# Attention of a hybrid layer: a third PSUM bank for the transposed probabilities, one bank for z and the way out, and their additions, statistics and shifts as steps of their own

## The chip, the cores and the metric

The kernel runs on one core of a Trainium2 chip. The metric is device time in microseconds (us), from the first to the last instruction of one execution and what lies around it; lower is better. Times of single instructions come from one profiled execution. A core has a matrix engine (PE, TensorE, with its weight loads shown apart as PEld), three engines for element-wise work (DVE = VectorE, ACT = ScalarE, POOL = GpSimd), and SP, whose queue issues most of the transfers. Matrix products land in PSUM, which has eight banks of 128 rows by 512 float32; DVE and ACT read them there.

## What is computed

One layer of a decoder, 1024 tokens of width 1024, float32:

```python
x = layer_norm(DN_ALPHA * x + 0.5 * swiglu(x, ffn1_wg[i], ffn1_wu[i], ffn1_wd[i]), ln1_g[i], ln1_b[i])
proj = x @ w_in[i]
o_gdn = gdn_mixer(g_q, g_k, g_v, g_z, g_b, g_a, ...)          # ends in o * rsqrt(...) * norm_w * silu(z)
o_nsa = nsa_mixer(n_q, n_kc, n_vc, n_ks, n_vs, n_kw, n_vw, n_gate, ...)
mix = jnp.concatenate([o_gdn, o_nsa], axis=-1) @ w_out[i]
x = layer_norm(DN_ALPHA * x + mix, ln2_g[i], ln2_b[i])
x = layer_norm(DN_ALPHA * x + 0.5 * swiglu(x, ffn2_wg[i], ffn2_wu[i], ffn2_wd[i]), ln3_g[i], ln3_b[i])
```

`nsa_mixer` is attention with 8 query heads of width 64 and 2 key heads, in three branches whose gated results are added: over 63 compressed blocks of keys, over all earlier keys (16 selected blocks of 64 are all blocks there are), and over a window of 512 keys. Each branch has its own softmax.

## The kernel before, in words

The kernel runs the first feed-forward part, then `project` (the projections and the gated DeltaNet), then `attend`, then the second feed-forward part. The change lies in `attend`, which does three things at once: the attention (`nsa_tile`), the z projection of the DeltaNet's gate (`z_blocks`), and the way out, that is the gate, the product with `w_out`, the residual and the statistics of the second layer norm (`tile_out`).

All float32 products are made of three products of rounded parts (a high part times both, a low part times the high one), so one step of z or of the way out is three matrix products of 128x512 (lines 1047 and 1093).

**The attention.** It goes through 8 tiles of 128 tokens, from the last (t = 7) to the first, and for each through two key heads (kv = 0, 1): 16 groups. A group has 1 + 8 or more units. A unit of the compressed branch makes scores of 4 heads against 64 blocks (lines 1658 and 1662); a unit of the other two branches makes the scores `sc` of one head against up to 512 keys (lines 1704 and 1705, and a mask at 1707), DVE takes their negated maximum `nm` (line 1709), and ACT the exponentials `pr` with their sum (line 1710). Scores have three banks. After the last unit of a branch DVE works out the factors `f` (lines 1720 to 1735) and POOL scales `pr` by them (line 1738), eight instructions for a group's branch. Some slots later come the branch's parts, one for each 128 keys: PE turns the probabilities of four heads round into the bank `pt` (line 1628, four products), ACT copies its high part `th` (line 1632), DVE the low part `tl` (line 1635), and PE adds both products with the values to `po` (line 1641). Then `po` is copied out (`ov`, line 1752), swapped by two transfers (`sw`) and added into the tile's output `o` by POOL (line 1761).

**The order.** `slot` puts one unit and one part together: first the turning of a part, then a unit's scores, then the low part and the exponentials, then the values' products of the part before. Between slots `run` takes steps of a filler at a fixed rate per group (line 1201). The filler is a generator, first `z_blocks`, then `tile_out(7)`, `tile_out(6)` and so on, each two tiles behind the attention; a step ends at each `yield`. When a tile's attention is through, for t below 6, the rest of the filler is run at once (line 1202). PE's order is the program's; the other engines' instructions are put in order by a scheduler that goes by what is ready and by the program's order. Each engine runs its own list in that order.

**z.** 8 blocks of 8 steps, each into a bank `pr` of the pool `zps`, which has two. After the eighth step ACT takes the tanh (line 1055), DVE forms (tanh + 1) * z (line 1056), ACT scales (line 1057) and SP stores it. These four have no step of their own: they are in the step that starts the next block.

**The way out.** `tile_out` loads the DeltaNet's output and z, POOL multiplies them (line 1071), ACT and DVE split the tile's output into `oh` and `ol` (line 1082, in `split`, lines 100 and 103), and PE makes two halves of eight steps each, again in the two banks of `zps`. DVE adds the residual to a half (line 1101), in the step after the first step of the next half. After the last step come one `yield`, the second addition, one more `yield`, and then in one go `ln_rows` (line 745): two `bn_stats`, `bn_aggr`, the reciprocal root `rstd` (DVE, then POOL, lines 108 and 110) and the shift `nmr` (DVE, line 749), which needs POOL's root. The eight banks are: `po` one, `pt` two, scores three, `zps` two.

## Time and profile before

| | |
|---|---|
| time, median of 3 runs | 2138.01 us (2135.66 to 2139.01) |
| the profiled execution's own time | 2137.25 us |
| its span, first to last instruction | 2135.3 us |
| PE, matrix products, busy in the span | 2074.9 us (97%) |
| DVE / ACT / POOL busy in the span | 1514.9 / 923.0 / 586.4 us |
| `attend` runs from about 1069 to 1475 us | 406 us |
| in it PE / DVE / ACT / POOL busy | 386.74 / 279.95 / 242.19 / 157.60 us |

PE's ends are modelled and its products overlap, so its busy time is read as an upper bound; what counts is how far one product starts after the other, and the idle time that the profile puts before a product with the instruction that ended it. That is a term in square brackets in the rows below. A product of 128x512 of the same kind starts 0.23 us after the one before where nothing holds it.

### The profile page before, as it was taken

To read this page: it belongs to the slowest core of one execution; us is meant where nothing else is said; L and a number is where in the kernel's file an instruction comes from. 1 tells how busy PE (TensorE), PEld (TensorE's weight loads), DVE (VectorE), ACT (ScalarE), POOL (GpSimd) and SP (SyncE) were. 2 spreads that over 40 slices of the span, in tenths; PEclk is the share of its full clock that TensorE was granted. 3 is DMA by queue.
4 is the path that set the end of the run, shared out by engine and by line. 5 is a ranking of instruction groups with operands and counts; after the bars stand their busy time and mean duration, and the time that the engine had idled before them with its cause. 6 is when DMAs were issued, how large, how long until landed. Compare 5 with 4: busy or idle time off the path is not lost.

```text
span 2135.3 us, 29714 instructions
## 1 busy us (share of the span) xinstructions
PE 2074.9 (97%) x10247; PEld 1712.8 (80%) x10247; DVE 1514.9 (71%) x2644; ACT 923.0 (43%) x1956; POOL 586.4 (27%) x608
## 2 busy tenths in 40 slices
PE   9999999999999999999999999999999999999998
PEld 7788888888887887888878777777788888887886
DVE  7867767587888648635557677765976556569998
ACT  6333333344443334245356666655533323334441
POOL 2544444200023013000014344442244444320011
PEclk9999999999999999999999999999999999999999
DMA  4345555198624524576455411122333223259761
GB/s 145 123 151 180 201 174 197 46 359 265 222 74 152 159 76 162 155 215 192 122 146 180 158 65 55 61 75 85 103 109 123 94 85 118 80 194 339 232 201 55
DMA packets 251384, 316.46 MB, mean 148 GB/s; under 512 B 25393, under 2 KB 154530, under 8 KB 251234
## 3 DMA queue, kind: packets, MB, share of 16 engines
q1 hardware_dynamic: 246498, 298.05, 42.9%
q0 software_dynamic: 4736, 16.52, 2.0%
q8 instruction: 81, 1.33, 0.3%
q14 instruction: 69, 0.57, 0.1%
HBM read 219.08 MB, written 93.32 MB: 146 GB/s over the span
## 4 chain that ended last, share of the span: by engine, by line
PE 38%; DVE 5%; issue 3%; DMA 2%; POOL 1%; ACT 1%; POOLq 0%; SPq 0%; DVEq 0%; ACTq 0%
PE bk L299 16%; PE dn L627 8%; PE pr L1093 4%; PE po L1641 3%; PE pt L1628 3%; PE pr L1047 2%; PE sc L1705 1%; PE sc L1704 1%; DVE tl L1635 1%; POOL pr L1738 1%; DVE st L278 0%; DVE wl L285 0%; DMA ba<-in_ln_b_dram 0%; PE sc L1707 0%; DMA zw<-zw 0%
## 5 line engine op out<-in xcount | busy, mean ns | idle before, releaser
L299 PE MATMUL bk<-x,wh 128*128 128x512 f32 x1040 | 325.1, 394 | 6.0 <-ACT wh L284 4.2
L627 PE MATMUL dn<-bl,ah 128*128 128x512 f32 x616 | 240.4, 390 | 1.2 <-DVE bl L103 1.2
L627 PE MATMUL dn<-bh,ah 128*128 128x512 f32 x616 | 239.9, 389 | 0.0
L627 PE MATMUL dn<-bh,al 128*128 128x512 f32 x616 | 239.8, 389 | 0.0
L299 PEld LDWEIGHTS bk<-x,wh 128*128 128x128 f32 x1040 | 196.7, 190 | 49.4 <-ACT wh L284 5.6
L299 PE MATMUL bk<-acc,wh 128*128 128x512 f32 x704 | 217.0, 389 | 0.4 <-ACT ev L233 0.2
L299 PE MATMUL bk<-t,wh 128*128 128x512 f32 x704 | 216.8, 389 | 0.0
L284 ACT CAST wh<-st 128x512 fp32r<-128x512 f32 x176 | 108.3, 622 | 240.9 <-PE bk L299 204.9
L299 PE MATMUL bk<-x,wl 128*128 128x512 f32 x520 | 204.8, 394 | 2.1 <-DVE wl L285 2.0
L356 POOL TENSOR_TENSOR ev<-ev 128x512 f32<-128x512 f32 x80 | 132.0, 1652 | 152.0 <-ACT wh L284 65.4
L100 ACT CAST ah<-raw 128x512 fp32r<-128x512 f32 x154 | 95.2, 622 | 175.5 <-PE dn L627 89.4
L284 ACT CAST wh<-wraw 128x512 fp32r<-128x512 f32 x130 | 80.3, 623 | 182.9 <-PE bk L299 172.3
L1738 POOL TENSOR_SCALAR pr<-pr,f 128x512 f32<-128x512 f32 (+3 forms) x192 | 106.8, 575 | 182.9 <-DMA zw<-zw 41.4
L299 PEld LDWEIGHTS bk<-acc,wh 128*128 128x128 f32 x704 | 132.0, 188 | 28.2 <-ACT ev L233 0.4
L299 PEld LDWEIGHTS bk<-t,wh 128*128 128x128 f32 x704 | 132.1, 188 | 27.5
L278 POOL TENSOR_TENSOR st<-wraw 128x512 f32<-128x512 f32 x76 | 101.0, 1329 | 183.8 <-DVE wl L285 151.7
L1709 DVE TENSOR_REDUCE nm<-sc 128x1 f32<-128x512 f32 (+3 forms) x192 | 99.2, 519 | 72.2 <-PE sc L1707 68.6
L285 DVE TENSOR_TENSOR wl<-wraw,wh 128x512 fp32r<-128x512 f32 x130 | 118.3, 914 | 36.0 <-ACT wh L284 36.0
L627 PEld LDWEIGHTS dn<-bl,ah 128*128 128x128 f32 x616 | 115.6, 188 | 27.1 <-DVE bl L103 3.2
L299 PE MATMUL bk<-acc,wl 128*128 128x512 f32 x352 | 136.9, 389 | 0.0
L299 PE MATMUL bk<-t,wl 128*128 128x512 f32 x352 | 136.9, 389 | 0.0
L627 PEld LDWEIGHTS dn<-bh,ah 128*128 128x128 f32 x616 | 115.7, 188 | 23.9
(390 smaller groups left out, 4783.6 us busy)
## 6 DMA issues: line engine op xcount, KB each, us to landing
raw<-h SPq DMA_DIRECT2D x154, 256.0 KB
raw<-in_ffn_wd_dram SPq DMA_DIRECT2D x154, 256.0 KB
h<-ev SPq DMA_DIRECT2D x140, 256.0 KB
wraw<-in_ffn_wg_dram SPq DMA_DIRECT2D x20, 1024.0 KB
wraw<-in_ffn_wu_dram SPq DMA_DIRECT2D x20, 1024.0 KB
wraw<-in_w_in_dram SPq DMA_DIRECT2D x20, 512.0 KB
acc<-in_x_dram SPq DMA_DIRECT2D x32, 256.0 KB
wo<-ev SPq DMA_DIRECT2D x32, 256.0 KB
```

Source lines behind the costliest of these rows:

```text
L100: nc.scalar.copy(hi, src)
L278: (e or u.adder).tensor_tensor(t, a, b, op=o)
L284: nc.scalar.copy(h, src)
L285: nc.vector.tensor_tensor(l, src, h.bitcast(F32), op=ALU.subtract)
L299: nc.tensor.matmul(ps, w[:, kc, :], v[kc], start=(kc == 0 and i == 0), stop=(kc == 3 and i == 2))
L356: (nc.vector if u.f + 2 == NF else nc.gpsimd).tensor_tensor(t, t, u.gate.g[i, j], op=ALU.mult)
L627: nc.tensor.matmul(ps, a[:, t * P:(t + 1) * P], w, start=start and i == 0, stop=stop and i == 2)
L1093: nc.tensor.matmul(pp, a[:, kc, :], w[u][:, kc, :], start=(kc == ks[0] and i == 0), stop=(kc == ks[-1] and i == 2))
L1628: nc.tensor.transpose(pt[:keys, h, :], pr()[:, h, c:c + keys], self.ident)
L1641: nc.tensor.matmul(po[0], v, w[:keys], start=(first and w is th[0]), stop=(last and w is tl[0]))
L1709: nc.vector.tensor_reduce(nm[:, j, h:h + 1], ps[:, :w], axis=AX.X, op=ALU.max, negate=True)
L1738: nc.gpsimd.tensor_scalar(prs[j][:, h, :], prs[j][:, h, :], f[:, j, h:h + 1], 1.0, op0=ALU.mult, op1=ALU.mult)
```

## The change

Five things are done. `zps` loses a bank and `npt` (the pool of `pt`) gains one. In `z_blocks` the four instructions behind a block become four steps (`finish`: the tanh, an empty step, DVE's product, the scaling with the store), so that a new block starts five steps after the last one ended. In `tile_out`, for tiles 7 to 2, a half's addition is a step of its own right behind its eighth step, and an empty one follows; the first half's `bn_stats` comes behind the first step of the second half. After the second half's addition come two empty steps, its `bn_stats`, the aggregate with the root, and the shift, a step each. `ln_rows` is cut into `ln_stats` and `ln_shift` for that. Tiles 1 and 0, which run when the attention is over, keep the addition one step behind and take a score bank for their second half. The rates of the filler rise, since there are more steps: from 20, 15, 15 and 14 to 28, 23, 23 and 22 for the first four groups, from 10 to 13 for the others.

```diff
--- before.py
+++ after.py
@@ -743,8 +743,10 @@
 
 
     def ln_rows(self, a, st=None, eps=LN_EPS):
+        return self.ln_shift(a, *self.ln_stats(a, st, eps))
+
+    def ln_shift(self, a, mv, rstd):
         nc = self.nc
-        mv, rstd = self.ln_stats(a, st, eps)
         nmr = self.cpool.tile([P, 1], F32, name="nmr", bufs=3)
         nc.vector.scalar_tensor_tensor(nmr, mv[:, 0:1], -1.0, rstd, op0=ALU.mult, op1=ALU.mult)
 
@@ -1012,10 +1014,10 @@
             self.nqs, self.npp = pool("nqs", bufs=2), pool("np", bufs=2)
             op, zp = pool("op", bufs=2), pool("zp", bufs=2)
             self.prs = Ring(*[(p, "pr") for p in reversed(prs)])
-            self.npo, self.npt = pool("npo", bufs=1, space=PSUM), pool("npt", bufs=2, space=PSUM)
-            sa, sb = pool("nsa", bufs=1, space=PSUM), pool("nsc", bufs=1, space=PSUM)
+            self.npo, self.npt = pool("npo", bufs=1, space=PSUM), pool("npt", bufs=3, space=PSUM)
+            sb, sa = pool("nsc", bufs=1, space=PSUM), pool("nsa", bufs=1, space=PSUM)
             self.nps = Ring((sb, "s0"), (sb, "s1"), (sa, "s2"))
-            self.zps = pool("zps", bufs=2, space=PSUM)
+            self.zps = pool("zps", bufs=1, space=PSUM)
             oT, fin = {}, {}
 
             loads = []
@@ -1037,6 +1039,17 @@
                     return w
 
                 w = [load(0, k) for k in range(2)]
+
+                def finish(u, b, pp):
+                    z = zp.tile([P, 512], F32, name="z", padded_shape=[P, T])
+
+                    def out():
+                        nc.scalar.mul(z, z, self.nw)
+                        nc.sync.dma_start(self.zT[b][:, u * 512:u * 512 + 512], z)
+
+                    return [lambda: nc.scalar.activation(z, pp, AF.Tanh), lambda: None,
+                            lambda: nc.vector.scalar_tensor_tensor(z, z, 1.0, pp, op0=ALU.add, op1=ALU.mult), out]
+
                 for n in range(8):
                     u, b = divmod(n, 4)
                     pp = self.zps.tile([P, 512], F32, name="pr")
@@ -1051,13 +1064,11 @@
                         if n == 0 and kc in (3, 5):
                             for br in range(2):
                                 self.nsa_keys(1, br, kc // 5, nk.tile([P, 2, 512], F32R, name=f"ks{br}{kc // 5}"))
-                    z = zp.tile([P, 512], F32, name="z", padded_shape=[P, T])
-                    nc.scalar.activation(z, pp, AF.Tanh)
-                    nc.vector.scalar_tensor_tensor(z, z, 1.0, pp, op0=ALU.add, op1=ALU.mult)
-                    nc.scalar.mul(z, z, self.nw)
-                    nc.sync.dma_start(self.zT[b][:, u * 512:u * 512 + 512], z)
                     if b == 3:
                         load_w(u)
+                    for f in finish(u, b, pp):
+                        f()
+                        yield
 
             def tile_out(t):
 
@@ -1081,10 +1092,13 @@
                 for ks in (slice(GH, ND), slice(0, GH)):
                     self.split(oh[:, ks], ol[:, ks], o[:, ks])
                     yield
-                add = None
+                st = self.cpool.tile([P, 2, 6], F32, name="bnst", bufs=2)
+                after = []
                 for u in range(2):
                     cs = slice(u * 512, u * 512 + 512)
-                    pp = self.zps.tile([P, 512], F32, name="pr")
+
+                    pp = (self.zps.tile([P, 512], F32, name="pr") if t > 1 or not u else
+                          sa.tile([P, 512], F32, name="sc", tag="s2"))
                     while loads:
                         loads.pop(0)()
                     ks = list(range(GH, ND)) + list(range(GH))
@@ -1093,17 +1107,23 @@
                             nc.tensor.matmul(pp, a[:, kc, :], w[u][:, kc, :], start=(kc == ks[0] and i == 0),
                                              stop=(kc == ks[-1] and i == 2))
                         yield
-                        if add is not None:
-                            add()
-                            add = None
-
+                        if after:
+                            after.pop(0)()
                     def add(pp=pp, cs=cs):
                         nc.vector.tensor_tensor(z[:, cs], pp, z[:, cs], op=ALU.add)
 
-                yield
-                add()
-                yield
-                fin[t] = self.ln_rows(z)
+                    if t > 1:
+                        add()
+                        yield
+                        yield
+                    else:
+                        after.append(add)
+                    after += [lambda u=u, cs=cs: nc.vector.bn_stats(st[:, u, :], z[:, cs])]
+                stats = []
+                for f in after + [lambda: stats.extend(self.ln_stats(z, st)), lambda: None]:
+                    yield
+                    f()
+                fin[t] = self.ln_shift(z, *stats)
 
             filler = []
 
@@ -1198,7 +1218,7 @@
                         g = groups.index((t, kv)) + 1
                         if g < len(groups):
                             nxt = group(g)
-                        run(us, (20, 15, 15, 14)[g - 1] / len(us) if g < 5 else 10 / len(us))
+                        run(us, (28, 23, 23, 22)[g - 1] / len(us) if g < 5 else 13 / len(us))
                     while t < 6 and fill():
                         pass
                     if t + 2 in (7, 6):
```

Where the instructions land is shown at three places. The first is on PE in the first group (t = 7, kv = 0), where the second block of z ends and the third begins; `pr<-xh,zw` is a step of z, `sc` are scores, `identb` a mask. Before:

```order
L1047 MATMUL pr<-xh,zw 128x512
L1704 MATMUL sc<-acc,qs 128x512
L1705 MATMUL sc<-acc,qs 128x512
L1707 LDWEIGHTS identb
L1707 MATMUL sc<-m_above,identb 128x128
L1047 MATMUL pr<-xh,zw 128x512
```

and in the changed kernel, where the lines left out are a second unit of scores like the first:

```order
L1060 MATMUL pr<-xh,zw 128x512
L1724 MATMUL sc<-acc,qs 128x512
L1725 MATMUL sc<-acc,qs 128x512
L1727 LDWEIGHTS identb
L1727 MATMUL sc<-m_above,identb 128x128
...
L1724 MATMUL sc<-acc,qs 128x512
L1725 MATMUL sc<-acc,qs 128x512
L1727 LDWEIGHTS identb
L1727 MATMUL sc<-m_above,identb 128x128
L1060 MATMUL pr<-xh,zw 128x512
```

One unit of scores stood between the two blocks, and the new block went into the other bank; now three units do, and the new block goes into the same bank.

The second is on ACT in the group t = 5, kv = 0, where the second half of the first tile's output is split (`oh<-o`); `pr,sm<-sc,nm` are exponentials with their sum, `th<-pt` is the high part of turned probabilities. Before:

```order
L1710 ACTIVATE pr,sm<-sc,nm 128x512
L1632 CAST th<-pt 128x512 x2
L1710 ACTIVATE pr,sm<-sc,nm 128x512
L100 CAST oh<-o 128x512
L1710 ACTIVATE pr,sm<-sc,nm 128x512
L1632 CAST th<-pt 128x512
L1710 ACTIVATE pr,sm<-sc,nm 128x512
L1710 ACTIVATE pr,sm<-sc,nm 128x256
```

Now:

```order
L1730 ACTIVATE pr,sm<-sc,nm 128x512
L1652 CAST th<-pt 128x512
L1730 ACTIVATE pr,sm<-sc,nm 128x512 x2
L1652 CAST th<-pt 128x512
L1730 ACTIVATE pr,sm<-sc,nm 128x512
L1730 ACTIVATE pr,sm<-sc,nm 128x256
L1652 CAST th<-pt 128x512
L1730 ACTIVATE pr,sm<-sc,nm 128x256
L100 CAST oh<-o 128x512
L1652 CAST th<-pt 128x512
```

The split stood behind two of the group's exponentials and stands behind six now.

The third is on DVE at the end of the group t = 5, kv = 1, where tile 7 ends; `cnm` is the first instruction of the next group, `z<-pr,z` the addition of the second half, `bnst`, `mv`, `rstd` and `nmr` the statistics. Before:

```order
L1101 TENSOR_TENSOR z<-pr,z 128x512
L1709 TENSOR_REDUCE nm<-sc 128x1
L729 BN_STATS bnst<-z 128x6
L1709 TENSOR_REDUCE nm<-sc 128x1
L731 BN_AGGR mv<-bnst 128x2
L103 TENSOR_TENSOR ol<-o,oh 128x512
L1635 TENSOR_TENSOR tl<-pt,th 128x512
L1720 TENSOR_TENSOR lo<-nm 128x4
L108 TENSOR_SCALAR rstd<-mv 128x1
L1665 TENSOR_REDUCE cnm<-sc 128x4
L1721 TENSOR_TENSOR nm<-lo,nm 128x8
L749 SCALAR_TENSOR_TENSOR nmr<-mv,rstd 128x1
```

Now, from the `bn_stats` of the second half on (its addition stands three maxima, a split and a low part earlier):

```order
L1121 BN_STATS bnst<-z 128x6
L1729 TENSOR_REDUCE nm<-sc 128x1 x3
L731 BN_AGGR mv<-bnst 128x2
L103 TENSOR_TENSOR ol<-o,oh 128x512
L1729 TENSOR_REDUCE nm<-sc 128x1
L108 TENSOR_SCALAR rstd<-mv 128x1
L1740 TENSOR_TENSOR lo<-nm 128x4
L1655 TENSOR_TENSOR tl<-pt,th 128x512
L751 SCALAR_TENSOR_TENSOR nmr<-mv,rstd 128x1
L1685 TENSOR_REDUCE cnm<-sc 128x4
```

The shift `nmr` stood behind `cnm` and stands ahead of it, and from the addition to the shift there are seven maxima now where there were two.

## Rows read from the trace of the kernel before

**Rows 1.** The page: the span, PE's busy time, and the chain of work that ended last, by line.

```profile
span 2135.3 us, 29714 instructions
...
PE 2074.9 (97%) x10247; PEld 1712.8 (80%) x10247; DVE 1514.9 (71%) x2644; ACT 923.0 (43%) x1956; POOL 586.4 (27%) x608
...
PE bk L299 16%; PE dn L627 8%; PE pr L1093 4%; PE po L1641 3%; PE pt L1628 3%; PE pr L1047 2%; PE sc L1705 1%; PE sc L1704 1%; DVE tl L1635 1%; POOL pr L1738 1%; DVE st L278 0%; DVE wl L285 0%; DMA ba<-in_ln_b_dram 0%; PE sc L1707 0%; DMA zw<-zw 0%
```

**Rows 2.** The waits of SP's queue from 1380 to 1500 us, who waited for whom: us in total, times, longest us. Line 253 loads weights of the second feed-forward part.

```profile
SPq L253 <- PE pr L1093: 15.1, 1, 15.1
```

**Rows 3.** The waits of PE in `attend` (1069 to 1475 us): us in total, times, longest us.

```profile
PE pt L1628 <- DVE tl L1635: 5.3, 9, 1.5
PE sc L1704 <- ACT pr L1710: 3.3, 2, 2.6
PE pt L1628 <- DVE rstd L108: 2.6, 2, 1.5
PE sc L1704 <- DVE pc L1667: 2.5, 1, 2.5
PE po L1641 <- DVE tl L1635: 2.0, 3, 1.5
...
PE pt L1628 <- DVE csm L1677: 0.5, 1, 0.5
```

**Rows 4.** PE in order of time, one slot without filler (t = 5, kv = 0): start us, us, engine, line, operation, out<-in.

```profile
1238.12 0.60 PE L1628 MATMUL pt<-ident,pr 128*128 128x128 f32 x4
...
1239.38 0.60 PE L1628 MATMUL pt<-ident,pr 128*128 128x128 f32 x4
```

**Rows 5.** The groups of DVE and then of ACT in `attend`: line, engine, operation, out<-in, count | busy us, mean ns of one | idle us before, and what ended it.

```profile
L1635 DVE TENSOR_TENSOR tl<-pt,th 128x512 fp32r<-128x512 f32 (+1 forms) x148 | 100.8, 681 | 13.3 <-ACT th L1632 11.7
L1709 DVE TENSOR_REDUCE nm<-sc 128x1 f32<-128x512 f32 (+3 forms) x192 | 99.2, 519 | 72.2 <-PE sc L1707 68.6 <-PE sc L1705 2.7
...
L1710 ACT ACTIVATE pr<-sc,nm 128x512 f32<-128x512 f32 (+3 forms) x192 | 106.5, 556 | 62.9 <-DVE nm L1709 54.1 <-POOL pr L1738 3.4 <-DVE f L1728 1.3
```

**Rows 6.** PE in order of time at the start of the group t = 4, kv = 0: what waits, and in brackets the idle time before it and what ended it.

```profile
1253.51 0.63 PE L1628 MATMUL pt<-ident,pr 128*128 128x128 f32 x4 [1.12 <-DVE rstd L108]
1253.90 0.47 PE L1641 MATMUL po<-th,acc 128*128 128x512 f32 x1
1254.21 0.39 PE L1641 MATMUL po<-tl,acc 128*128 128x512 f32 x1
1255.41 0.63 PE L1628 MATMUL pt<-ident,pr 128*128 128x128 f32 x4 [0.81 <-DVE tl L1635]
```

**Rows 7.** DVE in order of time at the same place.

```profile
1250.00 0.69 DVE L1101 TENSOR_TENSOR z<-pr,z 128x512 f32<-128x512 f32 x1 [0.32 <-PE pr L1093]
...
1250.94 0.68 DVE L729 BATCH_NORM_STATS2 bnst<-z 128x6 f32<-128x512 f32 x1
...
1251.86 0.20 DVE L731 BATCH_NORM_AGGREGATE mv<-bnst 128x2 f32<-128x12 f32 x1
...
1252.69 0.68 DVE L1635 TENSOR_TENSOR tl<-pt,th 128x512 fp32r<-128x512 f32 x1
...
1253.36 0.14 DVE L108 TENSOR_SCALAR rstd<-mv 128x1 f32<-128x1 f32 x1
...
1254.17 0.16 DVE L749 SCALAR_TENSOR_TENSOR nmr<-mv,rstd 128x1 f32<-128x1 f32 x1 [0.27 <-POOL rstd L110]
```

**Rows 8.** ACT in order of time in the group t = 5, kv = 0.

```profile
1203.14 0.70 ACT L1710 ACTIVATE pr<-sc,nm 128x512 f32<-128x512 f32 x1
...
1206.89 0.62 ACT L100 CAST oh<-o 128x512 fp32r<-128x512 f32 x1 [2.97 <-POOL o L1071]
```

**Rows 9.** POOL in order of time, there and, from 1244 us on, in the group t = 5, kv = 1.

```profile
1201.31 4.32 POOL L1738 TENSOR_SCALAR pr<-pr,f 128x256 f32<-128x256 f32 x8 [5.94 <-PE pt L1628]
1205.60 1.26 POOL L1071 TENSOR_TENSOR o<-o,zT 128x512 f32<-128x512 f32 x1
...
1244.08 4.54 POOL L1738 TENSOR_SCALAR pr<-pr,f 128x512 f32<-128x512 f32 x8 [11.17 <-PE pt L1628]
1248.75 1.55 POOL L1761 TENSOR_TENSOR o<-ov,sw 64x256 f32<-64x256 f32 x2
...
1253.58 0.56 POOL L110 TENSOR_TENSOR rstd<-rstd,mhalf 128x1 f32<-128x1 f32 x1 [1.36 <-DVE rstd L108]
```

**Rows 10.** Stretches, each a line: start and end us, the share of PE, PEld, DVE, ACT and POOL as busy us (instructions), the granted clock of PE as a share of its higher level, the share of the transfer engines, GB/s.

```profile
1076.00:1079.60 3.60, 3.60 (x10) 2.62 (x11) 2.64 (x7) 3.21 (x8) 0.00 (x0) 0.55 0.87 226
...
1208.00:1212.50 4.50, 4.05 (x17) 3.22 (x18) 3.33 (x6) 3.87 (x13) 1.28 (x1) 0.66 0.98 340
...
1309.00:1312.00 3.00, 3.00 (x13) 2.18 (x12) 2.19 (x10) 1.18 (x2) 0.72 (x2) 0.52 0.45 180
```

**Rows 11.** All engines in order of time where the second block of z ends: its last product, its tanh, and DVE's product.

```profile
1095.23 0.39 PE L1047 MATMUL pr<-xh,zw 128*128 128x512 f32 x1
...
1095.66 0.60 ACT L1055 ACTIVATE z<-pr 128x512 f32<-128x512 f32 x1 [1.24 <-PE pr L1047]
...
1096.79 0.68 DVE L1056 SCALAR_TENSOR_TENSOR z<-z,pr 128x512 f32<-128x512 f32 x1
```

**Rows 12.** PE in order of time at the end of the group t = 6, kv = 1, where no filler is left.

```profile
1194.14 0.44 PE L1704 MATMUL sc<-ks,qs 128*128 128x384 f32 x1 [0.67 <-ACT pr L1710]
...
1195.80 0.27 PE L1658 MATMUL sc<-mcmp,identb 128*128 128x256 bf16 x1 [0.53 <-ACT pr L1710]
```

## The prediction

> **What bounds the kernel now.** I read the page first: PE is busy for 97% of the span, and the chain that ended last runs mostly over PE's lines, those of `attend` among them [rows 1]. So the end moves by what PE idles, and time saved in `attend` reaches the end: the second feed-forward part's weights are issued when the last product of the way out (line 1093) is done [rows 2], so they move with it. Only `attend` is touched. There the waits of PE come next [rows 3]: 8.4 us before a turning into `pt` (5.3 + 2.6 + 0.5), 5.8 before scores (3.3 + 2.5), 2.0 before the values' products, 16.2 in all. Three stretches then show what the waits leave behind: after an idle time of over 2 us, or two shorter ones in a row, the granted clock fell to 0.52 to 0.66, so products ran at or near the lower of its two levels (1.2 GHz instead of 2.4). That cost 3.6 * 0.45 + 4.5 * 0.34 + 3.0 * 0.48 = 4.6 us [rows 10]. About 21 us is therefore all that can be won by better order, 1% of the time.
>
> A slot without filler takes PE 1239.38 - 1238.12 = 1.26 us with 256 keys [rows 4]; DVE needs about 0.68 for a low part and 0.52 for a maximum, ACT 0.56 and more for an exponential [rows 5]. So PE sets the pace even there, and falls behind only where DVE, ACT or POOL have a burst of other work.
>
> **The change part by part.** No engine gets other work: the same products, additions and statistics run, in another order, so the sum is one of waits. Signs: plus is gained.
>
> *A, the third bank of `pt`.* It lets a turning go ahead without the low part of two turnings before. But behind the turning come the values' products of the part before, which need that part's own low part. In [rows 6] the turning waits 1.12 us until 1253.51, and the second product of the values starts at 1254.21; its low part was ready at 1252.69 + 0.68 = 1253.37 [rows 7]. With the bank free PE would reach it at about 1253.4 and go on: 0.7 to 0.8 us are won. The next wait in the same row, 0.81, isn't won again, since that product then waits for the next low part. So the twelve waits of [rows 3] (9 + 2 + 1, 8.4 us) return at most about 0.7 each where they stand alone and half of that in pairs. I take +5; the bounds are 0 (DVE's lateness moves whole to the values' products) and +8.4.
>
> *B, the split of tile 7's output on ACT.* ACT stood for 2.97 us before `oh` [rows 8], because POOL multiplied the output by z only after eight scalings (1201.31 + 4.32, then 1.26 to 1206.86) [rows 9]. The exponentials behind it held the score banks, and PE idled 2.6 us, the longest of its waits for scores [rows 3]; the clock then cost 4.5 * 0.34 = 1.5 [rows 10]. In the changed order `oh` stands four exponentials and more later; with a slot of at least 0.9 to 1.3 us each ACT gets there some 4 us later than 1203.9, when POOL is done. Gain up to 4.1; bound below 0, if POOL is late by as much. I take +3.5, since POOL's order there is unchanged.
>
> *C, statistics and shift.* At the end of tiles 7 and 6, the addition, two statistics, the root and the shift took DVE about 1.9 us in 4.3 [rows 7], beside the next group's first work, and PE waited there. They now lie earlier, in the last units of the group. DVE's sum over the stretch without filler stays; what goes is a part of the pile, and with it perhaps the second fall of the clock (3.0 * 0.48 = 1.4 [rows 10]). Against it: the shift needs POOL's root, which stands behind eight scalings and two swaps (4.54 + 1.55 + 0.56 = 6.65 us after `f` [rows 9]). DVE's own work between `f` and the shift is seven maxima, three other instructions of 0.7 and small ones, about 6, so DVE may stand up to 0.7 at each of two places. I take +1; bounds -1.4 and +2.
>
> *D, one bank for z.* A new block waits for DVE's product of the last one. From the last product of a block to the end of that instruction took 1096.79 + 0.68 - 1095.23 = 2.24 us [rows 11]. PE covers this with what now stands between: at two of seven places three units of scores, 3 * 0.46 (two products at 0.23) + 0.23, so 0.6 is open at each; at the others with two to four whole slots of 1.26 [rows 4], so nothing. The way out's halves are covered in the same manner. I take -1. If the tanh comes late the bound is the whole length each time, 7 * (2.24 - 0.23) = -14; above, 0.
>
> *E, the start.* The first scores wait 2.5 us for DVE's first work [rows 3]. One more step of z (three products, 0.7 us) now stands ahead of that wait: +0.7, bounds 0 and, if the clock then doesn't fall, 0.7 + 3.6 * 0.45 = +2.3.
>
> *F, group ends without filler.* Where the last units of a group have no filler beside them, scores come faster than ACT's exponentials free the banks: 0.67 + 0.53 = 1.2 us at the one such end of before [rows 12]. After the change three ends look like that, (6, 1), (5, 1) and (4, 1), since a tile's last step of products lies six slots earlier. So -2.4; bounds 0 and -5.
>
> *G, the late tiles.* Steps of the way out come in pairs and end earlier in a group, and DVE's statistics lie at the boundary as before. No row prices it; the nearest is the 2.0 us of waits for values' products [rows 3]. I take -0.5, bounds -2 and +2.
>
> Sum: 5 + 3.5 + 1 - 1 + 0.7 - 2.4 - 0.5 = 6.3 us. The profiled execution took 2137.25, so 2131.0; the median of the runs is 0.76 above that execution, so 2131.7.
>
> **The rivals.**
> 1. *The waits only move.* PE runs behind DVE at the places of A; the third bank then lets it walk 0.4 us further and stop at the values' products. For it speaks that the 2.0 us there stand next to the same bursts. A gives 0.5, B 1, C 0, the rest stays: 0.5 + 1 + 0 - 1 + 0.7 - 2.4 - 0.5 = -1.7, so 2139.7.
> 2. *The single bank of z stops PE; slower.* Place: the seven ends of blocks. The tanh stands in ACT's list behind exponentials, the product in DVE's behind maxima. With three exponentials of 0.56 + 0.2 ahead the 2.24 become 4.5. Then 2.9 us are open at the two short places and about 1.5 at three others, 10.3 in all, and two falls of the clock at 1.6 each (as in [rows 10]) make 13.5 in place of 1: 6.3 - 12.5 = -6.2, so 2144.2. It decides from about 10 us on, that is from a length of about 4 us. Against it: the measured length was 2.24 with the same neighbours [rows 11]. The Trainium skill speaks for this rival: "Perfetto Trace Analysis", section "Matmuls", says that independent groups of products should rotate through different banks, so that the reading of one overlaps the next group's products. The rows so far bear it out only where less than 2 us of other products lie between two blocks.
> 3. *The third bank gives back all its waits.* If DVE catches up because scores reach it earlier, A is 8.4 and C 2: 6.3 + 3.4 + 1 = 10.7, so 2127.3. Against it stands the second wait in [rows 6]. The Trainium skill, "Perfetto Trace Analysis", section "Optimization Strategy", reads a gap that repeats on the engine that should be busy as a lack of buffers, which would be this case; the trace agrees for the turnings alone.
>
> **How the numbers follow.** Chances: my forecast 0.50 (2127.5 to 2134.5), rival 1 0.25, rival 2 0.13, rival 3 0.12. A measurement of this kernel can tell about 0.2% from no change, 4.3 us: faster is below 2133.7, slower above 2142.3. Faster: 0.43 of the forecast's 0.50 and rival 3, 0.55; slower: rival 2 and 0.02 of rival 1 for the ends of F and G, 0.15; the same: 0.30. The range takes in rival 3 and rival 1 with their bounds and leaves out rival 2 and the lowest gains: 2125 to 2141. The predicted time is the forecast's, 2131.7.
>
> **What would show it.** A: turnings that wait for `tl` or `rstd` are nearly gone, and waits of line 1661 for `tl` rise from 2.0 to some 4 us; were they to rise by 8, rival 1 holds. B: no wait of some 3 us before `oh` near 1205 us, and the clock there stays full. C: the wait of `nmr` for POOL's root, 0.27 in [rows 7], is under 1 us. D: waits of line 1060 for DVE's product of z sum to about 1 us; over 8 would be rival 2. F: scores wait for exponentials at the ends of three groups, some 1.2 us each. `attend` should end about 6 us sooner, and everything after it should shift by the same. The prediction is wrong if PE's waits stay at 16 us in sum under other names, or if POOL's scalings, whose places beside the slots move, make ACT or DVE stand where they didn't.

## The result and the profile after

The changed kernel took 2125.58 us in the median of 6 runs (2123.69 to 2129.52), the kernel before 2138.51 beside it. The ratio is 0.9944, with a 95% interval of 0.9933 to 0.9954, so 12.0 us less (9.8 to 14.3). A second measurement, on the chip of the last experiments, gave 0.9947 (0.9935 to 0.9960).

The page of the changed kernel answers to [rows 1]; the lines of `attend` that are named here have numbers higher by 11 to 20, but for the end of a block of z (tanh 1050, DVE's product 1051, scaling 1047).

```profile
span 2122.0 us, 29657 instructions
...
PE 2066.4 (97%) x10247; PEld 1707.1 (80%) x10247; DVE 1511.4 (71%) x2644; ACT 921.6 (43%) x1956; POOL 589.1 (28%) x608
```

PE has the same 10247 products and is busy for 8.5 us less; its mean granted clock over the span is 0.995, and was 0.990. The waits of PE in `attend` (1069 to 1464 us; us in total, times, longest) answer to [rows 3]:

```profile
PE po L1661 <- ACT ov L1772: 5.4, 9, 1.0
PE po L1661 <- DVE tl L1655: 2.0, 4, 0.9
PE sc L1724 <- DVE pc L1687: 1.8, 1, 1.8
PE pr L1060 <- DVE z L1051: 1.0, 2, 0.8
PE pr L1060 <- DMA zw<-zw: 1.0, 1, 1.0
```

No turning (L1648) waits now, where they had waited 8.4 us, and no score waits for an exponential. The values' products still wait 2.0 us for their low part. New are two waits for DVE's product of z, 1.0 us, and nine waits of a group's first values' product for ACT's copy of `po`, 5.4 us; the kernel before had one of these:

```profile
PE po L1641 <- ACT ov L1752: 0.4, 1, 0.4
```

Of the stretches that answer to [rows 10] the first still has the lower clock; the places of the second and the third run at the full one (columns as there):

```profile
1076.80:1080.40 3.60, 3.60 (x11) 2.78 (x10) 2.29 (x6) 2.62 (x8) 0.00 (x0) 0.53 0.98 261
1196.00:1212.00 16.00, 15.78 (x101) 13.12 (x102) 13.58 (x33) 12.67 (x34) 7.08 (x11) 1.00 0.80 286
...
1295.00:1312.00 17.00, 15.94 (x95) 12.47 (x96) 12.67 (x37) 10.39 (x30) 11.74 (x21) 1.00 0.38 117
```

DVE at the end of a tile of the way out, in order of time, answers to [rows 7]. Addition, statistics and shift now stand apart with maxima and low parts between them, and the shift waits 0.82 for POOL's root:

```profile
1241.45 0.69 DVE L1113 TENSOR_TENSOR z<-pr,z 128x512 f32<-128x512 f32 x1
...
1244.83 0.68 DVE L1121 BATCH_NORM_STATS2 bnst<-z 128x6 f32<-128x512 f32 x1
...
1246.96 0.20 DVE L731 BATCH_NORM_AGGREGATE mv<-bnst 128x2 f32<-128x12 f32 x1
...
1249.91 0.16 DVE L751 SCALAR_TENSOR_TENSOR nmr<-mv,rstd 128x1 f32<-128x1 f32 x1 [0.82 <-POOL rstd L110]
```

ACT's `oh`, which answers to [rows 8], stands at 1210.00 and waits 1.21 there in place of 2.97, and PE has no wait behind it. POOL's product, which it waits for, now stands 1.58 us for the transfer of z and no longer directly behind the scalings:

```profile
1208.68 1.29 POOL L1082 TENSOR_TENSOR o<-o,zT 128x512 f32<-128x512 f32 x1 [1.58 <-DMA zT<-zT]
...
1210.00 0.62 ACT L100 CAST oh<-o 128x512 fp32r<-128x512 f32 x1 [1.21 <-POOL o L1082]
```

**Where the new waits come from.** Below is PE in order of time at the end of the group (7, 1), after the change. The last product into `po` starts at 1159.32, three products of scores follow, and then the next group's first product needs `po`, which ACT is still copying:

```profile
1159.32 0.39 PE L1661 MATMUL po<-tl,acc 128*128 128x512 f32 x1
1159.55 0.28 PE L1724 MATMUL sc<-acc,qs 128*128 128x256 f32 x1
...
1160.73 0.50 PE L1661 MATMUL po<-th,VC 64*128 64x512 f32 x1 [0.71 <-ACT ov L1772]
```

ACT at that place: a scaling of z and an exponential are ahead of the copy.

```profile
1159.03 0.73 ACT L1047 ACTIVATE z<-z,cols 128x512 f32<-128x512 f32 x1 [0.28 <-DVE z L1051]
1159.66 0.46 ACT L1730 ACTIVATE pr<-sc,nm 128x256 f32<-128x256 f32 x1
...
1160.11 0.57 ACT L1772 COPY ov<-po 128x512 f32<-128x512 f32 x1
```

The kernel before, same place: a step of the filler lies between, with three products (0.7 us), and PE doesn't wait.

```profile
1158.18 0.39 PE L1641 MATMUL po<-tl,acc 128*128 128x512 f32 x1
1158.41 0.40 PE L1047 MATMUL pr<-xh,zw 128*128 128x512 f32 x1
...
1159.51 0.49 PE L1641 MATMUL po<-th,VC 64*128 64x512 f32 x1
```

The change has more steps in the filler, and many of them hold no product: four at a block of z, some nine in a row between two tiles. Where a group ends among these, PE meets the copy with only scores to do: at eight of the nine waits no product of the filler lies between the two groups.

**An account of the time.** For it I took each product of PE from its own start to the next one's start, less the lower quartile for its shape, as its loss, and put losses of over 0.15 us down to what released the wait. That includes, at each wait, some 0.2 us that the view of waits leaves out (the expectations below call it excess). The stretch is from the first product of z to the first product of line 627, in the second feed-forward part, which holds the same work in every kernel. All numbers are us of one profiled execution each; e1 to e6 are experiments below.

| loss of PE | before | after | e1 | e6 | e3 | e4 |
|---|---|---|---|---|---|---|
| turnings | 10.5 | 0 | 0 | 8.9 | 0 | 0 |
| values' products, low part | 2.7 | 3.2 | 6.2 | 0.5 | 3.2 | 6.2 |
| a group's first, copy of `po` | 0.6 | 7.1 | 1.6 | 5.8 | 3.5 | 4.5 |
| scores, exponentials | 4.3 | 0 | 5.1 | 0 | 4.3 | 0.3 |
| z and way out, DVE's product | 0 | 1.4 | 8.8 | 1.4 | 3.8 | 1.7 |
| start | 2.7 | 2.0 | 2.7 | 1.5 | 2.7 | 2.0 |
| weights of z (DMA) | 2.1 | 1.2 | 0.7 | 3.6 | 3.0 | 2.2 |
| rest: clock, small, second feed-forward | 40.3 | 35.3 | 41.4 | 35.9 | 36.2 | 36.0 |
| length of the stretch | 842.4 | 829.4 | 845.7 | 836.8 | 836.0 | 832.2 |

The waits for the weights of z go from 0.7 to 3.6 among these kernels with no edit of theirs near them, so differences of 2 us in this stretch are not read.

### The profile page after: what moved, and what is told of

It is laid out like the page before. It is cut to its first block, busy times and chain, and to the rows that moved or that the text cites. A ratio compares the mean times of both kernels' runs of the same rounds, so it can differ in the third digit from the quotient of the medians.

```text
span 2122.0 us, 29657 instructions
## 1 busy us (share of the span) xinstructions
PE 2066.4 (97%) x10247; PEld 1707.1 (80%) x10247; DVE 1511.4 (71%) x2644; ACT 921.6 (43%) x1956; POOL 589.1 (28%) x608
```

## The experiments

**Theory 1:** the third bank of `pt` returns the waits before turnings, and the steps are there so that one bank of z is enough. **Theory 2:** the bursts of DVE and ACT are the cause; spreading them helps, and a bank only lets PE walk on to the next wait. Later, for the new waits at `po`, **F1:** they are time lost, **F2:** PE only stands there instead of elsewhere.

### e1: the banks alone

```
 # kernel before
-self.npo, self.npt = pool("npo", bufs=1, space=PSUM), pool("npt", bufs=2, space=PSUM)
+self.npo, self.npt = pool("npo", bufs=1, space=PSUM), pool("npt", bufs=3, space=PSUM)
...
-self.zps = pool("zps", bufs=2, space=PSUM)
+self.zps = pool("zps", bufs=1, space=PSUM)
```

> The kernel before with three banks for pt and one for z and the way out; no step is split and the rates are the old ones. Theory 1 (the third bank by itself returns the waits before turnings, 11.1 us of excess in the trace of before; the steps are there only so that one bank of z is enough): PE has no wait before a turning, waits for z's product at the ends of blocks and of the way out's halves take 2 to 4 us, so about 8 us faster than before, 2130. Theory 2 (the bursts of DVE and ACT are the cause, and spreading them is what helps; the bank only lets PE walk on to the next wait): the waits go over to the values' products, 8 us or more there, and with the waits at z the time is 2138 to 2142, not faster than before.

Measured: 1.0021 of before (1.0012 to 1.0030), 4.5 us slower. PE's waits:

```profile
PE pr L1047 <- DVE z L1056: 4.6, 6, 1.4
PE po L1641 <- DVE tl L1635: 4.3, 7, 1.5
...
PE pr L1093 <- DVE z L1101: 2.4, 2, 2.0
```

Neither theory holds alone. The turnings' waits are gone (8.4 us), a third of their loss returns at the values' products (from 2.7 to 6.2), and one bank for z and the way out costs 8.8 where their ends stand in one step. This is the place that rival 2 of the prediction names, but not its cause: from a block's last product to the end of DVE's product it took 1.74 to 2.65 us here, where the rival asked for about 4. The next block only follows too soon. The Trainium skill ("Perfetto Trace Analysis", section "Matmuls") says that groups of products should rotate through banks so that reading one overlaps the next. The trace agrees here, with 7.0 us of waits; with the steps between two blocks it agrees for 1.0 us only.

### e2 and e6: the steps with two banks of `pt`

e2 has two banks for z, e6 one, and a bank of PSUM unused.

```
 # changed kernel, e2 and e6
-self.npo, self.npt = pool("npo", bufs=1, space=PSUM), pool("npt", bufs=3, space=PSUM)
+self.npo, self.npt = pool("npo", bufs=1, space=PSUM), pool("npt", bufs=2, space=PSUM)
 # e2 alone
-self.zps = pool("zps", bufs=1, space=PSUM)
+self.zps = pool("zps", bufs=2, space=PSUM)
```

> The changed kernel with the banks of before: two for pt, two for z and the way out; all steps and rates of the change stay. Theory 1 (the bank): the waits before turnings are back with 8 us or more, the late split of tile 7's output keeps its 3.5 us, so 2133 to 2136. Theory 2 (the steps): waits before turnings are under 4 us, and the time is 2126 to 2130.

> The changed kernel with two banks for pt and one for z; one bank of PSUM is left unused, all else stays. Theory 1 (A is the bank's): waits before turnings of 7 to 8 us are back and 3 us before values' products go, so 4 to 5 us more than the changed kernel, 2130 to 2131. Theory 2 (the steps alone are enough, and the bank only moves the wait): within 1.5 us of the changed kernel, 2125 to 2127. If a single bank of z costs PE little once its end is in steps, this kernel is within 2 us of the one with the steps alone.

Measured: e2 0.9980 (0.9971 to 0.9988), e6 0.9979 (0.9969 to 0.9988). Once a block ends in steps, the second bank of z is worth nothing that can be measured. From e6 to the changed kernel, 0.9979 to 0.9944, the third bank brings 0.35%, about 7 us; of the 7.4 us between the two in the table above, 2.4 are waits for the weights of z, which are not read. Both times are above what theory 2 asked. Theory 1's waits came (8.9 us of loss in e6); its times were 1.4 us too long for e2 and as much too short for e6. PE in e6:

```profile
PE pt L1648 <- DVE tl L1655: 5.6, 8, 1.7
PE po L1661 <- ACT ov L1772: 4.5, 7, 1.0
```

The turnings wait for low parts again; those for statistics (2.6 in [rows 3]) don't come back, so these were ended by the steps and their rates.

### e3: the end of a block of z in one step

```
                     for f in finish(u, b, pp):
                         f()
-                        yield
...
-run(us, (28, 23, 23, 22)[g - 1] / len(us) if g < 5 else 13 / len(us))
+run(us, (20, 15, 15, 14)[g - 1] / len(us) if g < 5 else 13 / len(us))
```

> The changed kernel, but the end of a block of z (tanh, product, scaling, store) is issued in one step again, and the rates of the first four groups are those of before; three banks for pt and one for z. Theory 1: a new block follows at once, so its first product waits for the product of the last one, at up to seven places 0.5 to 1 us, some 4 us more than the changed kernel, 2130. Theory 2 (the empty steps are of use because they spread the bursts): 6 us or more, 2132. If the empty steps cost more at group ends than they save, 2123 to 2126.

Measured: 0.9982 (0.9973 to 0.9991), 2131.85 us, near what theory 2 said, for another reason:

```profile
PE pr L1060 <- DVE z L1051: 3.1, 5, 1.4
PE sc L1723 <- ACT pr L1729: 3.1, 3, 2.1
```

The waits at z are those that theory 1 named. But the wait of scores behind `oh` is back as well (ACT stands 3.3 us for POOL's product with z):

```profile
1213.14 0.62 ACT L100 CAST oh<-o 128x512 fp32r<-128x512 f32 x1 [3.34 <-POOL o L1081]
```

So term B hangs on z's steps and their rates, which put `oh` later, and not on the way out's steps (e4).

### e4: the way out as before

Addition, statistics, root and shift as in the kernel before, 10 steps in place of 13; z's steps and the banks stay.

```
...
-    after += [lambda u=u, cs=cs: nc.vector.bn_stats(st[:, u, :], z[:, cs])]
-for f in after + [lambda: stats.extend(self.ln_stats(z, st)), lambda: None]:
-    yield
-    f()
-fin[t] = self.ln_shift(z, *stats)
+yield
+add()
+yield
+fin[t] = self.ln_rows(z)
...
-run(us, (28, 23, 23, 22)[g - 1] / len(us) if g < 5 else 13 / len(us))
+run(us, (28, 23, 23, 22)[g - 1] / len(us) if g < 5 else 10 / len(us))
```

> The changed kernel, but additions, statistics, root and shift of a tile of the way out are issued as in the kernel before, with the old rate of the last groups (10 steps in place of 13); z in steps and the banks of the change stay. Theory 1: the third bank covers the pile of statistics too, so 1 to 2 us more than the changed kernel, 2127. Theory 2: the pile stops the values' products for 1 us and more at tiles 7 to 5, with a fall of the clock, 4 us or more over the changed kernel, 2130 and above.

Measured: 0.9957 (0.9943 to 0.9970), 2127.91 us; 2 to 3 us above the changed kernel, with intervals that overlap. In waits:

```profile
PE po L1653 <- DVE tl L1647: 4.3, 7, 1.5
PE po L1653 <- ACT ov L1764: 3.6, 5, 1.0
```

PE waits 2.3 us more before values' products (4.3, not 2.0) and 1.8 less at the copy of `po` (3.6, not 5.4). The pile and the old rate were not tried apart, so that the first comes from the pile and the second from the rate is likely and not shown. Theory 1 is the nearer one: the pile brought no fall of the clock (granted 1.00 in all of `attend`).

### e5: two banks for `po`

```
-self.npo, self.npt = pool("npo", bufs=1, space=PSUM), pool("npt", bufs=3, space=PSUM)
+self.npo, self.npt = pool("npo", bufs=2, space=PSUM), pool("npt", bufs=2, space=PSUM)
```

> The changed kernel with the third bank given to po: two for po, two for pt, one for z. It tells what the nine new waits of a group's first values' product for ACT's copy of po (7.1 us of excess in the trace of the changed kernel) are. Theory F1 (one bank of po, and nothing but three products of scores between the last product of a group and the first of the next): these waits are gone, and the waits before turnings return with some 8 us, less the 3.2 us before values' products: 2125 to 2129. Theory F2 (PE stands there only because ACT or DVE are behind, so the wait goes over to the next one): they go over into other waits at the same places, and with the turnings' waits on top the time is 2132 or more.

Measured: 0.9972 (0.9961 to 0.9983), 2130.95 us, between what the two theories said. No wait for the copy of `po` is left, where e6, which differs in this bank alone, has 4.5 us of them; but the two times can't be told apart (0.9972 and 0.9979). The turnings wait longer, and PE waits at places where e6 has no wait.

```profile
PE pt L1648 <- DVE tl L1655: 6.6, 8, 1.5
...
PE sc L1724 <- ACT pr L1730: 0.5, 2, 0.4
...
PE pt L1648 <- DVE lo L1753: 0.4, 1, 0.4
PE pt L1648 <- DVE lo L1752: 0.3, 1, 0.3
```

With two banks of `pt`, then, F2 is the nearer one, though a gain of some 1.5 us (0.9979 - 0.9972) is not ruled out.

### e7: a product forced to each end of a group

```
...
 slot(unit)
 debt += rate
+while self.soon:            # the last product into po was just issued
+    debt -= 1
+    if fill() in (False, 2):    # 2: the step held products
+        break
```

> The changed kernel, but where a group's last values' product was just issued, filler steps are taken until one with three products of z or of the way out has come (the steps are taken from the following slots' share); banks, steps and rates stay. Theory F1 (the copy of po takes about 1.06 us from the last product's start, and three scores cover 0.4 of it): three products more, 0.69 us, cover most of each of the nine waits, 0.8 us in the mean, so 4 to 6 us less than the changed kernel, 2120 to 2122. Theory F2 (the time is only moved, since the products are missing in the slots behind): within 1.5 us of the changed kernel. A third way, worse: the steps that are taken earlier put the tanh and the split ahead of exponentials, and waits for scores return, 2128.

Measured: 0.9991 (0.9979 to 1.0002), 2135.28 us: worse than the changed kernel. The waits at `po` fell from 5.4 to 2.3 us, but in the late tiles the forced steps brought the way out's products directly behind the split that they need:

```profile
PE pr L1107 <- DVE ol L103: 4.0, 2, 2.3
```

After the first of these the granted clock was 0.60 for 8 us, after the second 0.51 for 6.5:

```profile
1380.40:1388.50 8.10, 8.00 (x31) 6.20 (x32) 4.84 (x12) 3.27 (x9) 7.12 (x10) 0.60 0.44 157
...
1416.00:1422.50 6.50, 6.50 (x27) 5.39 (x26) 4.34 (x12) 2.70 (x9) 5.78 (x11) 0.51 0.65 211
```

A third stretch at a low clock follows a wait of 0.77 us for the copy of `po` and one of 0.43 for an exponential:

```profile
1296.50:1303.50 7.00, 7.00 (x33) 6.34 (x32) 5.36 (x16) 3.53 (x11) 4.25 (x4) 0.51 0.69 208
```

Together the three cost 7.00 * 0.49 + 8.10 * 0.40 + 6.50 * 0.49 = 9.9 us, about as much as e7 lies above the changed kernel (0.9991 - 0.9944, 10 us). The profiled execution is the slowest of e7's twelve (2126.65 to 2138.64 us), so the others need not have had all three; but the median of their granted clocks is low too, 0.992 where the changed kernel has 0.995.

### e8 and e9: the way out one group earlier

```
...
+if kv and 5 <= t + 1 < NT:            # tiles 7, 6, 5; the others as they were
+    filler.append(tile_out(t + 1))
...
-run(us, (28, 23, 23, 22)[g - 1] / len(us) if g < 5 else 13 / len(us))
+run(us, (24, 24, 26, 26)[g - 1] / len(us) if g < 5 else 13 / len(us))
 # e9 also: the loop of e7, for the first three groups
```

> The changed kernel, but the way out of tiles 7, 6 and 5 is put on the filler list one group earlier and the rates of the first four groups are 24, 24, 26, 26 in place of 28, 23, 23, 22: the run of steps without products lies between the ends of groups, and a step with three products stands between the last product of a group and the first of the next at five of the first seven places in place of two. Nothing is forced. Theory F1: three of the nine waits for the copy of po (0.8, 0.7 and 1.0 us in the trace of the changed kernel) go, nothing comes: 2 to 3 us less than the changed kernel, 2123. Theory F2 (a product step there is missing elsewhere): within 1 us of the changed kernel, 2125 to 2127. A third way: the output of tile 7 is split four steps earlier and ACT stands behind POOL's scalings again, as in the kernel before (3 us and a fall of the clock): 2129 to 2131.

> As the run with the way out earlier, and beside it, in the first three groups alone, steps of z are taken behind a group's last values' product until one with three products has come. Theory F1: one more of the waits for the copy of po (0.9 us) goes, so 0.5 to 1 us less than that run, 2122. Theory F2: no less than that run. The third way of that run holds here too.

Measured: e8 0.9967 (0.9955 to 0.9980), e9 0.9968 (0.9957 to 0.9980), both some 5 us above the changed kernel (against its second measurement the intervals overlap a little). In e8 the waits at `po` fell to 1.9 us, more than F1 asked, and others took their place: the third way, though with PE itself waiting for `oh`.

```profile
PE pr L1107 <- ACT oh L100: 2.1, 1, 2.1
...
PE pt L1650 <- POOL pr L1760: 0.7, 2, 0.3
```

In e9 the waits at `po` fell further, to 1.2 us, with no gain over e8, as F2 said.

### e10 to e12: the cover in three groups, no empty step, the changed kernel again

e10 is the changed kernel with the loop of e7 for the first three groups. e11:

```
-return [lambda: nc.scalar.activation(z, pp, AF.Tanh), lambda: None,
+return [lambda: nc.scalar.activation(z, pp, AF.Tanh),
...
-run(us, (28, 23, 23, 22)[g - 1] / len(us) if g < 5 else 13 / len(us))
+run(us, (26, 21, 21, 20)[g - 1] / len(us) if g < 5 else 13 / len(us))
```

> The changed kernel, with the smallest form of the cover: in the first three groups, behind a group's last values' product, steps of z are taken until one with three products has come; the way out starts where it did and the rates stay. It touches two of the nine waits for the copy of po (0.8 and 0.9 us). Theory F1 (each covered wait is time won): both go and nothing comes, 1 to 2 us less than the changed kernel that runs beside it. Theory F2 (the wait goes over into the next one, as in the run with the way out earlier): the same as the changed kernel within 1 us, with new waits of about 1.5 us between 1085 and 1190 us.

> The changed kernel without the empty step between the tanh and the product of z, three steps at the end of a block in place of four, and 26, 21, 21, 20 steps in the first four groups. The chain from a block's last product over the tanh to the end of DVE's product took 2.24 us in the trace of before, and two steps more take about 2.4 us of slots. Theory 1 (the steps are needed to cover that chain): waits of a block's first product for DVE rise from 1.4 to 4 us, 2 to 3 us more than the changed kernel. Rival (three steps are enough, the empty one only thins the filler): within 1 us of the changed kernel, or 1 us less.

> The changed kernel itself, for comparison on the same chip: 0.9944 of the kernel before by the first measurement, 2125.6 us.

Measured side by side: e10 0.9946 (0.9934 to 0.9958), e11 0.9944 (0.9930 to 0.9957), the changed kernel 0.9947 (0.9935 to 0.9960). They can't be told apart. In e10 the waits at `po` fell from 5.1 in e12 to 3.7, those at z rose from 1.0 to 1.6:

```profile
PE po L1664 <- ACT ov L1775: 3.7, 6, 1.0
...
PE pr L1060 <- DVE z L1051: 1.6, 3, 0.8
```

The stretch of the account was 2.3 us shorter in e10 (827.9, not 830.2), the time 0.01% less; whether F1 holds for two waits is below what can be measured. The 2.3 us need not come from the waits: in e12 the granted clock was 0.50 from 1077.60 to 1081.00 and from 1483.80 to 1490.60 us, in e10 it was 1.00 at the first of these places and low for half as long at the second (0.51 from 1482.20 to 1485.70). In e11 z's waits stayed at 1.0 us, so the empty step isn't needed.

## Why the prediction was right in kind and too small

It said 6.3 us less, and 12.0 were measured: the direction held, and the time, 2125.58, lies at the low end of the range, outside the forecast's own 2127.5 to 2134.5. `attend` ended 11.0 us sooner, not 6 (its last product started at 1472.44 before, at 1461.42 after). The account before and after, by the prediction's terms:

- **A and C, taken as 5 + 1.** The turnings' loss went from 10.5 to 0, that of the values' products rose by 0.5 only: 10.0 in sum. This is the step that failed, by size. From e6 to the changed kernel the bank gives 8.9 - 2.7 = 6.2, of which 7.1 - 5.8 = 1.3 returns at `po`; A's 5 is near that, though A expected the waits for low parts (2.0) to rise to some 4, and they stayed at 2.0. The other 3.8 come with the steps, from the kernel before to e6: 1.6 at the turnings (the waits for statistics go, shorter ones come) and 2.2 at the values' products. C had 1 for all of that, as a small part of the pile. A was priced from one place in [rows 6], where only the high part's product stands between a turning and the product that needs the low part. e1 shows what C does for A: with the pile in place 6.2 us were lost at the values' products, and 3.2 without it (e4: 6.2).
- **B, taken as 3.5.** The loss of scores went from 4.3 to 0; e1 and e3 have it, and e2, e6 and e4 (0.3) don't.
- **D, taken as -1.** Measured -1.4. Rival 2 decides from a length of about 4 us on, from a block's last product to the end of DVE's product; it was 1.74 to 2.84 us in the changed kernel, so the rival's condition didn't come. The 8.8 of e1 stand at no greater length, so they don't price the rival.
- **E, taken as +0.7.** Measured 2.7 to 2.0. The clock fell there as before; in e4 and e10, which start in the same way, it didn't (see the last section for e4).
- **F and G, taken as -2.4 and -0.5.** Ends without products came, but the place was wrong: no score waits for an exponential, while the first values' product waits for the copy of `po`, -6.5 in place of -2.9. I had priced the chain over the score banks and not the single bank of `po`.
- **The clock, counted only inside B and C.** The row "rest" fell by 5.0. In the profiled pair the clock fell to 1.2 GHz six times in this stretch before and twice after, at about 1.6 us each by the starts of the products. The falls at the two places in `attend` are gone. Behind `attend` there were three, then one; but that part is only 1.8 us shorter (440.15, then 438.35), since two waits for `ev` grew by 1.7 there. Nothing was edited in it, and the other traces have from none (e3, e8) to three (e1, e4, e7) falls in it, so these 1.8 can't be put down to the change. Over all runs the median of the granted clock is 0.993 for the kernel before (69 runs; the profiled execution, 0.990, is at their lower end) and 0.995 for the changed one (11 runs). That is 0.002 * 2130, some 4 us by estimate. It is 0.993 in e1, 0.994 in e2 and 0.995 in e6, which points to the steps and not to the bank.

With the weights of z (+0.9) this sums to 10.0 + 4.3 - 1.4 + 0.7 - 6.5 + 5.0 + 0.9 = 13.0, the difference of the two stretches. Against 6.3 that is 6.7 more: 4.0 in A and C, 0.8 in B, 5.0 in the clock and 0.9 in the weights, less 0.4 in D and 3.6 in F and G. That the time fell inside the range is partly luck: had F and G cost what they were priced at, it would lie near 2122, below the range.

Rival 3 came nearest in time (2127.3), and its 8.4 + 2 for A and C is near the 10.0, but its cause doesn't hold: only 6.2 of these come with the third bank. In e1, where it was paid for with the second bank of z and no steps stood between, the kernel got slower; with the steps it brings about 7 of the 12 us. Rival 1 falls with the turnings' waits: 6.2 of their 8.9 us didn't come back at the values' products.

The shape of it is an interaction: banks alone +0.21%, steps alone -0.20%, both -0.56%. The steps make the z bank spare, and the spare bank pays as the third of `pt`. Open is what the waits at `po` are worth with three banks of `pt`: e7 to e9 cut them by 3 us and more and lost that elsewhere, e10 cut them by 1.4 and shows no difference in time. A first product held back by a slot wasn't tried.

## What to carry to other kernels

Where PSUM is full, ask which bank can be made spare by putting other products between the last product of one block and the first of the next, so that the bank is read meanwhile, and do both edits together: here the bank alone lost 0.21%, the steps alone gained 0.20%, and both gained 0.56%. Price a freed buffer at every place where its wait stands, by what PE has between the waiting instruction and the next one that needs the same producer. Filler steps without products are not free: look where runs of them fall, above all at the ends of groups where a single bank is handed over.

## What was not expected of the hardware

The same wait didn't always lower the clock. In the second feed-forward part PE waits 2.0 us for DVE's `wl` in both kernels; behind it the granted clock was 0.60 before (1550 to 1554 us) and 1.00 after (1538.5 to 1542.5):

```profile
1550.00:1554.00 4.00, 4.00 (x13) 3.16 (x12) 3.84 (x6) 2.53 (x5) 1.28 (x1) 0.60 0.12 43
```

```profile
1538.50:1542.50 4.00, 4.00 (x18) 3.29 (x18) 3.84 (x6) 2.37 (x5) 1.11 (x1) 1.00 0.17 65
```

The first scores of `attend` show it again. In the changed kernel they wait 1.84 us for DVE, and the granted clock behind that was 0.53 (the stretch from 1076.80 us in the section on the result); in e4, whose edits all lie later, they wait as long, and it was 1.00. The wait in the changed kernel, then in e4, and e4's stretch behind it:

```profile
1076.13 0.47 PE L1724 MATMUL sc<-acc,qs 128*128 128x512 f32 x1 [1.84 <-DVE pc L1687]
```

```profile
1076.94 0.47 PE L1716 MATMUL sc<-acc,qs 128*128 128x512 f32 x1 [1.84 <-DVE pc L1679]
```

```profile
1076.80:1080.40 3.60, 3.46 (x15) 2.87 (x16) 2.64 (x7) 3.44 (x8) 0.00 (x0) 1.00 0.94 283
```

So a fall costs 1.6 us (4.00 * 0.40) in one execution and nothing in another, and single profiles of kernels this close differ by that much without an edit at the place.
